# Placing the operands of the large matrix products at a fixed address distance in a two-layer decoder trunk

## The chip, the cores and the metric

The kernel runs on one core of one Trainium2 chip. The metric is the device time of one execution in microseconds. Three timed runs of the kernel before gave 616.25, 617.42 and 618.36 us; the median is 617.42 us.

## The reference, cut to what matters

One sequence of 256 tokens by 1024 features passes two layers. Layer 0 mixes tokens with causal attention (16 heads of 64), layer 1 with an mLSTM (8 heads); each is followed by a SwiGLU feed-forward part of width 2816. All of it is float32.

```python
def swiglu(xn, w_gate_up, w_down):
    gu = jnp.einsum('bsd,df->bsf', xn, w_gate_up)
    g, u = gu[..., :D_FF], gu[..., D_FF:]
    return jnp.einsum('bsf,fd->bsd', jax.nn.silu(g) * u, w_down)
...
    for i in range(DEPTH):
        j = i // N_MIXERS
        if i % N_MIXERS == 0:
            h = h + moba_mixer(rmsnorm(h, attn_norm[j]), attn_w_qkv[j], attn_w_o[j], cos, sin)
        else:
            h = h + mlstm_mixer(rmsnorm(h, mlstm_norm[j]), mlstm_w_in[j], mlstm_b_gates[j],
                                mlstm_head_norm[j], mlstm_w_out[j])
        h = h + swiglu(rmsnorm(h, ffn_norm[i]), ffn_w_gate_up[i], ffn_w_down[i])
    return rmsnorm(h, final_norm)
```

## The kernel before

Every float32 factor a is split exactly into a high part and a low part of the type float32r, and a product is made of three matmuls, high by high, high by low and low by high (`mm3`, line 176, through `mm`, line 173, so that nearly all matmuls have line 174). The weights come as 196 units of [128, 1024] in the order of use: the DMA queue of SP fills one of four buffers `raw`, ScalarE (ACT) casts it to `wh`, VectorE (DVE) subtracts to get `wl` (`prefetch`, line 139; `low`, line 135). There are eight buffers each of `wh` and `wl`. A unit feeds 24 matmuls of 256 columns or 12 of 512.

A matmul has a stationary operand (128 columns, brought in by a weight load, the engine PEld in the profile) and a moving operand (256 or 512 columns here). Which side the weights are on differs by phase:

- `first_block` (line 246) and `pair_block` (line 235): the weights are stationary and the normalised input `xh`, `xl` moves, 256 columns. This is the query/key part of both mixers (units `aqk`, `mqk`) and all gate and up products (`gu0`, `gu1`). In each feed-forward part `first_block` makes 192 matmuls and 18 chunks of `pair_block` make 48 each, 1056 together; they write tiles `ps`, one chunk per layer a tile `acc`.
- `out_tiles` (line 330): weights stationary, 256 columns move: `oh`, `ol` after attention (`ao`), `yh`, `yl` after the mLSTM (`mout`), `hh`, `hl` in the down product of layer 0 (`d0`), 24 matmuls a K tile. They write tiles `acc`.
- `tok_block` (line 267, the value and gate inputs `av`, `mv`, `mo`) and `tok_tiles` (line 393, the down product `d1` of layer 1): the input or `hh`, `hl` is stationary and the weights move, 512 columns, 12 matmuls a unit or K tile.

In the two mixer phases the work of the heads (small matmuls, softmax, gates) is put between steps of the large products at places written down by hand (`Stream`, line 279). In the feed-forward phases the chunks and the down products follow each other: a chunk of 48 matmuls, then a K tile of the down product. The order on TensorE is the order of the code; that on the other engines is written out in the attention phase and made by the scheduler elsewhere.

Where tiles lie in the on-chip memory SBUF follows from the sizes of the pools and tiles, one behind the other. Of interest is the start of an operand within 256 bytes; all offsets inside these tiles that the large products use are multiples of 512 bytes. In the built program before:

| operand | start, bytes modulo 256 |
|---|---|
| `xh`, `xl` | 0 |
| `wh`, `wl` | 32 |
| `hh`, `hl`; `oh`, `ol` | 224 |
| `yh`, `yl` | 32 |

So the distance D, start of the stationary operand less start of the moving one, modulo 256, is 32 in `first_block` and `pair_block`, 64 in `d0` and `ao`, 0 in `mout`, 224 in `tok_block` and 192 in `d1`.

Of the kernel before, what the change touches and what calls it, by code (L numbers as in the profile page):

```python
# [9 lines left out]
F32 = mybir.dt.float32  # L10
F32R = mybir.dt.float32r
# [5 lines left out]
P = 128  # L17
S = 256
NF = 8
NJ = 22  # L20
EPS = 1e-6
# weights: units prepared ahead, buffers, K tiles between a hidden tile and its use
LOOK = 4
# [6 lines left out]
WARM = 16  # L30
# where the pieces of the heads come, in steps of the large products
A_D1, A_X, A_D2, A_N, A_D3, A_L, A_D4, A_O1, A_O2 = 0.5, 1, 3, 1, 1, 1.5, 0.5, 1, 1
# [3 lines left out]

# columns of the constant tables
C_COS, C_SIN, C_AMASK, C_ID = 0, 256, 512, 768
C_EMASK, C_TRIU, C_TRIS, C_ID2, C_END = 896, 1152, 1280, 1408, 1416
# columns of the small vectors  # L40
V_ATTN, V_FFN0, V_MLSTM, V_FFN1, V_HEAD, V_BIAS, V_END = 0, 8, 16, 24, 32, 40, 56


def unit_names():
    """The order in which the units of weights (name, index, half) are used."""
    def each(name, ids):
        return [(name, i, h) for i in ids for h in range(2)]

    def outer(name):
        return [(name + "*", k, 0) for k in range(NF)]  # L50

    def a_units():
        n, v = [], each("av", range(4))
        parts = {0: [v[0:4]], 1: [v[4:4 + V1 // 4], v[4 + V1 // 4:]]}
        for i in ORDER:
            n += parts[i].pop(0) if i < 4 else each("aqk", [i])
        return n

    def ffn(l):
        n = outer(f"gu{l}")  # L60
        nd = 0
        for j in range(4, NJ):
            while nd <= j - LAG and j >= 6:
                n.append((f"d{l}", nd // 2, nd % 2))
                nd += 1
            n += each(f"gu{l}", [j])
        return n + [(f"d{l}", i // 2, i % 2) for i in range(nd, NJ)]

    n = outer("aqk") + a_units() + each("ao", range(4)) + ffn(0)
    n += outer("mqk") + each("mv", (0, 1)) + each("mo", (0, 1)) + each("mv", (2, 3)) + each("mo", (2, 3))  # L70
    n += each("mout", range(4)) + ffn(1)
    return n
# [3 lines left out]
def trunk_kernel(ctx: ExitStack, tc: tile.TileContext, x, w, wg, fw, tab, out):  # L76
    nc = tc.nc
    names = unit_names()
    index = {n: i for i, n in enumerate(names)}

    const = ctx.enter_context(tc.tile_pool(name="const", bufs=1))
    raw_pool = ctx.enter_context(tc.tile_pool(name="raw", bufs=RAW))
    w_pool = ctx.enter_context(tc.tile_pool(name="wsplit", bufs=WBUFS))
# [21 lines left out]
    nc.scalar.activation(dummy, warm[:, 0:1], AF.Exp)  # L105

    XV = xp.tile([P, V_END + NF * S], F32, name="XV")
    vt = XV[:, 0:V_END]
    X = XV[:, V_END:].rearrange("p (f t) -> p f t", f=NF)
    tab_t = const.tile([P, C_END], F32, name="tab_t")  # L110

    # weights: a stream of units [128, 1024], split exactly into two float32r parts
    raws = []
    split = {}
# [24 lines left out]
    def prefetch(upto, lag=0):  # L139
        for c in range(len(split), min(upto, len(names))):  # L140
            load(c + RAW - 1)
            wh = w_pool.tile([P, 1024], F32R, name="wh", tag="wh")
            wl = w_pool.tile([P, 1024], F32R, name="wl", tag="wl")
            split[c] = (wh, wl)
# [31 lines left out]
    def mm3(o, a, b, start, stop):  # L176
        """o += a^T b for exactly split a = (ah, al), b = (bh, bl)."""
        mm(o, a[0], b[0], start, False)
        mm(o, a[0], b[1], False, False)
        mm(o, a[1], b[0], False, stop)  # L180

    class Norm:
        """The split x * w, and the row scale 1/rms that is applied to what the products give."""

# [13 lines left out]
        def square(self, f):  # L198
            """Squares of the tiles f and f + 1."""
            xs = X[:, f:f + 2].rearrange("p f t -> p (f t)")  # L200
# [18 lines left out]
        def rows(self):  # L219
            pb = acc_tile()  # L220
            for t in range(2):
                nc.tensor.transpose(pb[:, t * P:(t + 1) * P], self.r[:, t:t + 1].to_broadcast([P, P]), ident)
            self.R = sm.tile([P, S], F32, name="R", tag="R")
            nc.scalar.copy(self.R, pb[:, 0:S])
# [10 lines left out]
    def pair_block(name, i, n, bank):  # L235
        """Products of one [8K, 2 x 128] chunk, 128 features by 256 tokens each."""
        for k in range(NF):
# [8 lines left out]
    def first_block(name, n):  # L246
        """The first four chunks of a phase with the K tiles outermost: the products start as soon as the
        first K tile of x is there."""
        banks = [ps_tile() for _ in range(4)]
# [17 lines left out]
    def tok_block(name, i0, n, evict, later):  # L267
        """x-stationary product [tokens, 512 columns] over two chunks."""
        banks = [acc_tile() for _ in range(2)]
# [9 lines left out]
    class Stream:  # L279
        """The large products of a phase in small steps, between which the work of the heads is put: each  # L280
        piece at the number of steps that it comes after."""

# [13 lines left out]
        def when(self, pos, ready, f, *args):  # L296
            """f at pos, or after it as soon as ready() holds."""
            def attempt():
# [31 lines left out]
    def out_tiles(acc, u, rhs, first, last, fs=range(NF)):  # L330
        """acc[f] += W[f]^T rhs for one K tile."""
        for f in fs:
# [4 lines left out]
    def out_steps(acc, name, i, src):  # L337
        """The output products of K tile i in four steps."""
        u, rhs = unit(name, i // 2, i % 2), src.pop(i)
# [4 lines left out]
    def out_start(acc, name, src):  # L344
        """The output products of the first two K tiles, by two banks at a time."""
        steps = []
# [14 lines left out]
    def finish(acc, steps, col):  # L361
        """The last output products, by bank, and the next norm's operands as the banks end."""
        n = Norm(col)
# [12 lines left out]
    def tok_tiles(acc, u, h, t, c, last):  # L376
        """acc[t, c] += h^T W for one K tile, tokens by features."""
        sl, cs = slice(t * P, (t + 1) * P), slice(c * 512, (c + 1) * 512)
        mm3(acc[2 * t + c], (h[0][:, sl], h[1][:, sl]), (u[0][:, cs], u[1][:, cs]), False, last)

    def finish_last(acc, steps, fwb, fp):
        """The last output products and the final norm, tokens by features."""
        for t in range(2):
# [21 lines left out]

# [1 line left out]
    n = n0 = Norm(V_ATTN)  # L407
# [19 lines left out]
    def stacks(pool, mv, bufs, ubufs=2, later=None):  # L427
        """mv: [m | a] of two heads. Per head [[mh, ah, ml], [ml, al, mh]], so that two products over the
        128 rows give all of a^T m."""
        u = pool.tile([P, 1024], F32R, name="u", tag="u", bufs=ubufs)  # L430
# [22 lines left out]
    with ExitStack() as actx:  # L453
# [5 lines left out]
        nc.gpsimd.tensor_mul(Cr, tcos, n.R)  # L459
        nc.gpsimd.tensor_mul(Sr, tsin, n.R)  # L460
        VT = ap1.tile([P, 2, 16, P], F32R, name="VT")
        swap = [8 + i if i < 8 else i - 8 if i < 16 else i for i in range(32)]
# [19 lines left out]
        def v_evict(n0, banks, part=0):  # L482
            # per head pair [vh0, vl0, vl1, vh1]
            for t in range(2):
# [50 lines left out]
        def transposes(h):  # L535
            pt = pr.pop(h)
            tp = ps_tile()
            # (k0, q0), (k0, q1), (k1, q1)
            for i in range(3):
# [78 lines left out]

# [1 line left out]
    def ffn(l, n, fp, col):  # L620
# [25 lines left out]
        def down(j):  # L646
            u = unit(f"d{l}", j // 2, j % 2)
            if not acc:
                acc.extend(acc_tile() for _ in range(4))
                if last_phase:  # L650
                    # the residual seeds the sums
                    for b in range(4):
# [32 lines left out]

# [1 line left out]
    with ExitStack() as mctx:  # L687
        mp = mctx.enter_context(tc.tile_pool(name="ml", bufs=2))
        m1 = mctx.enter_context(tc.tile_pool(name="ml1", bufs=1))
        VV = m1.tile([P, 2, 8, 258], F32R, name="VV")  # L690
        nc.gpsimd.memset(VV[:, :, :, 128:129].bitcast(F32), 1.0)
# [11 lines left out]

        # gates
        gp = acc_tile()
# [20 lines left out]
        def gates_1():  # L726
# [16 lines left out]
            z = m1.tile([P, 2, 8], F32, name="gz")  # L743
            # log1p(e) = 2 atanh(e / (2 + e)), |e / (2 + e)| <= 1/3
            nc.vector.tensor_scalar(d, e, 2.0, None, op0=ALU.add)
# [47 lines left out]
        def heads_e(h):  # L793
# [3 lines left out]
            E = mp.tile([P, 384], F32, name="E", tag="E", bufs=2)  # L797
            # (s1, t1), (s0, t0), (s0, t1)
            for i, b in enumerate((1, 0, 2)):
# [21 lines left out]
        def heads_b(h, t):  # L821
            # h / sqrt(mean(h^2) + eps) with h = num / den is num / sqrt(mean(num^2) + eps den^2)
            if t == 0:
                hpre[h] = (mp.tile([P, 2, 129], F32, name="hpre", tag="hpre", bufs=2),
                           sm.tile([P, 8], F32, name="hsc", tag="hsc", bufs=3))
# [39 lines left out]
        def o_evict(i, banks):  # L865
            # sigmoid(v) = (1 + tanh(v / 2)) / 2
            rh = sm.tile([P, 2], F32, name="rh", tag="rh")
# [135 lines left out]
```

## Time and profile before

| | |
|---|---|
| median of three timed runs | 617.42 us |
| span of the profiled execution, first to last instruction | 614.8 us |
| TensorE busy with matmuls (PE) / weight loads (PEld) | 601.1 us (98%) / 571.5 us (93%) |
| VectorE / ScalarE / GpSimd busy | 417.1 us / 340.7 us / 76.9 us |
| matmuls in the trace | 4524 |
| share of the span on PE, chain that ended last | 80% |

The 2.6 us between span and median lie around the span, in the launch and its end. Matmuls are pipelined: the trace gives each a duration of some 0.28 us (256 columns), but they start closer together than that. What a product costs is the distance from one start to the next, and the chain that ended last, which counts a matmul from the start of one to the start of the next, shows it: its pieces give a start, a length and the number of instructions.

### The profile page before, as it was taken

How to read it: one execution, taken by the hardware profiler on the slowest of the kernel's cores; microseconds unless marked ns; L12 is line 12 of the kernel's file. 1: busy time of each engine (PE TensorE's matmuls, PEld its weight loads, DVE VectorE, ACT ScalarE, POOL GpSimd, SP SyncE). 2: the span in 40 equal slices, each digit the busy share in tenths (PEclk: the TensorE clock that was granted, in tenths of full speed). 3: DMA queues.
4: the chain of work that ended last, by engine and by line, in shares of the span. 5: the costliest groups of instructions: out<-in, count | busy, mean ns of one | idle time of the engine just before them, and what ended most of it. 6: DMA issues, size and time to landing. Idle time of an engine off the chain costs nothing.

```text
span 614.8 us, 11568 instructions
## 1 busy us (share of the span) xinstructions
PE 601.1 (98%) x4524; PEld 571.5 (93%) x4524; DVE 417.1 (68%) x663; ACT 340.7 (55%) x611; POOL 76.9 (13%) x76
## 2 busy tenths in 40 slices
PE   8997999999999999999999999999999999999995
PEld 7987999999999999999999778899999999999984
DVE  5899898788765656566477677867676565656532
ACT  7645999677544444444275368856564444444422
POOL 2573320051000000000032300112200000000000
PEclk9999999999999999999999999999999999999999
DMA  8878965558555556555528758442865565655401
GB/s 312 281 216 266 248 191 156 168 187 285 184 199 177 200 174 200 177 198 179 172 69 298 225 198 224 154 138 73 298 212 172 176 200 176 199 177 201 142 0 68
DMA packets 36342, 116.39 MB, mean 189 GB/s; under 512 B 4544, under 2 KB 7360, under 8 KB 36288
## 3 DMA queue, kind: packets, MB, share of 16 engines
q1 hardware_dynamic: 36288, 115.66, 58.2%
q8 instruction: 35, 0.57, 0.4%
q14 instruction: 19, 0.16, 0.1%
HBM read 105.15 MB, written 1.05 MB: 173 GB/s over the span
## 4 chain that ended last, share of the span: by engine, by line
PE 80%; DMA 5%; DVE 5%; issue 3%; ACT 3%; POOL 2%; SPq 2%; POOLq 0%; ACTq 0%; DVEq 0%
PE ps L174 44%; PE acc L174 34%; DMA raw<-w 4%; DVE wl L137 2%; DMA stk<-u 1%; PE ps L540 1%; DVE u L435 1%; ACT wh L147 1%; DVE xl L195 1%; ACT xh L194 1%; DVE mqk L700 0%; POOL gpoly L753 0%; POOL sh L472 0%; POOL qk L473 0%; SPq L439 0%
## 5 line engine op out<-in xcount | busy, mean ns | idle before, releaser
L137 DVE TENSOR_TENSOR wl<-raw,wh 128x1024 fp32r<-128x1024 f32 (+2 forms) x199 | 244.8, 1236 | 114.8 <-ACT wh L147 111.9
L147 ACT CAST wh<-raw 128x1024 fp32r<-128x1024 f32 (+2 forms) x199 | 205.4, 1038 | 195.1 <-PE ps L174 108.2
L174 PE MATMUL ps<-xh,wh 128*128 128x256 f32 x864 | 245.1, 284 | 0.6 <-ACT wh L147 0.6
L174 PE MATMUL ps<-xh,wl 128*128 128x256 f32 x864 | 243.9, 282 | 0.5 <-DVE wl L137 0.5
L174 PE MATMUL ps<-xl,wh 128*128 128x256 f32 x864 | 243.4, 282 | 0.0
L174 PEld LDWEIGHTS ps<-xh,wh 128*128 128x128 f32 x864 | 163.6, 189 | 1.6 <-ACT wh L147 0.8
L174 PEld LDWEIGHTS ps<-xl,wh 128*128 128x128 f32 x864 | 163.8, 190 | 0.7
L174 PEld LDWEIGHTS ps<-xh,wl 128*128 128x128 f32 x864 | 163.6, 189 | 0.9 <-DVE wl L137 0.9
L174 PE MATMUL acc<-hh,wh 128*128 128x256 f32 x176 | 48.9, 278 | 0.0
L174 PE MATMUL acc<-hl,wh 128*128 128x256 f32 x176 | 48.8, 277 | 0.0
L174 PE MATMUL acc<-hh,wl 128*128 128x256 f32 x176 | 48.7, 277 | 0.0
L207 POOL TENSOR_TENSOR ssum<-ssum,sq 128x512 f32<-128x512 f32 x12 | 20.8, 1735 | 204.2 <-issue 169.4
L629 DVE TENSOR_TENSOR tgu<-ps,R 128x512 f32<-128x512 f32 x42 | 28.6, 690 | 23.8 <-PE ps L174 23.8
L174 PE MATMUL acc<-wh,xh 128*128 128x512 f32 x96 | 39.4, 411 | 0.0
L174 PE MATMUL acc<-wl,xh 128*128 128x512 f32 x96 | 38.0, 395 | 0.0
L174 PE MATMUL acc<-wh,xl 128*128 128x512 f32 x96 | 37.9, 395 | 0.0
L174 PE MATMUL acc<-wh,hl 128*128 128x512 f32 x88 | 34.7, 394 | 0.0
L174 PE MATMUL acc<-wl,hh 128*128 128x512 f32 x88 | 34.5, 392 | 0.0
L174 PE MATMUL acc<-wh,hh 128*128 128x512 f32 x88 | 34.2, 389 | 0.0
L174 PEld LDWEIGHTS acc<-hh,wh 128*128 128x128 f32 x176 | 33.2, 188 | 0.0
L174 PEld LDWEIGHTS acc<-hh,wl 128*128 128x128 f32 x176 | 33.1, 188 | 0.0
L174 PEld LDWEIGHTS acc<-hl,wh 128*128 128x128 f32 x176 | 33.0, 188 | 0.0
(179 smaller groups left out, 853.4 us busy)
## 6 DMA issues: line engine op xcount, KB each, us to landing
raw<-w SPq DMA_DIRECT2D x195, 512.0 KB, 3.4
stk<-u SPq DMA_DIRECT2D x24, 192.0 KB, 4.4
stk<-u SPq DMA_DIRECT2D x24, 128.0 KB, 4.3
stk<-u SPq DMA_DIRECT2D x24, 64.0 KB, 3.7
out<-yout SPq DMA_DIRECT2D x4, 256.0 KB, 2.2
XV<-x SPq DMA_DIRECT2D x7, 128.0 KB, 6.2
tab_t<-tab SPq DMA_DIRECT2D x1, 708.0 KB, 6.9
fwb<-fw SPq DMA_DIRECT2D x1, 512.0 KB, 3.4
```

The costliest lines, as they stand in the source:

```text
L137: nc.vector.tensor_sub(wl[:, sl], raws[c][:, sl], wh[:, sl].bitcast(F32))
L147: nc.scalar.copy(wh[:, sl], raws[c][:, sl])
L174: nc.tensor.matmul(o, lhsT=lhsT, rhs=rhs, start=start, stop=stop, skip_group_check=True)
L194: nc.scalar.activation(self.h[:, f], X[:, f], AF.Copy, scale=wc)
L195: nc.vector.scalar_tensor_tensor(out=self.l[:, f], in0=X[:, f], scalar=wc, in1=self.h[:, f].bitcast(F32), op0=ALU.mult, op1=ALU.subtract)
L207: nc.gpsimd.tensor_add(self.ssum, self.ssum, sq)
L435: nc.vector.tensor_sub(u[:, 512:1024], mv, u[:, 0:512].bitcast(F32))
L540: nc.tensor.transpose(tp[:, i * P:(i + 1) * P], pt[:, i * P:(i + 1) * P], ident)
L629: nc.vector.tensor_mul(t.rearrange("p (g t) -> p g t", g=2), bank.rearrange("p (g t) -> p g t", g=2), n.R2())
```

## The change

The tiles are moved so that D is 64 in all of the large products. Four things do this: unused pad tiles of 56, 56, 8, 16 and 48 float32 per partition push later tiles on, each with a memset of one column on GpSimd; the buffers of `wh` and `wl` have 1088 columns instead of 1024, of which the units whose weights move (`av`, `mv`, `mo`, `d1`) use 1024 from column 32 on and the others from column 0; the tile `R` has one buffer instead of two; the rows of `hpre` are 144 long instead of 129. Comments are removed, which shifts the line numbers.

```diff
+MOVING = ("av", "mv", "mo", "d1")
...
     const = ctx.enter_context(tc.tile_pool(name="const", bufs=1))
+    pad_pool = ctx.enter_context(tc.tile_pool(name="pad", bufs=1))
+
+    def pad(pool, n):
+
+        t = pool.tile([P, n], F32, name=f"pad{len(pads)}", bufs=1)
+        nc.gpsimd.memset(t[:, 0:1], 0.0)
+        pads.append(t)
+
+    pads = []
+    pad(pad_pool, 56)
...
+    pad(xp, 56)
+    pad(sm, 8)
     XV = xp.tile([P, V_END + NF * S], F32, name="XV")
...
-            wh = w_pool.tile([P, 1024], F32R, name="wh", tag="wh")
-            wl = w_pool.tile([P, 1024], F32R, name="wl", tag="wl")
+            o = 32 if names[c][0] in MOVING else 0
+            wh, wl = (w_pool.tile([P, 1088], F32R, name=a, tag=a)[:, o:o + 1024] for a in ("wh", "wl"))
...
-            self.R = sm.tile([P, S], F32, name="R", tag="R")
+            self.R = sm.tile([P, S], F32, name="R", tag="R", bufs=1)
...
+        pad(ap1, 16)
         VT = ap1.tile([P, 2, 16, P], F32R, name="VT")
...
+        pad(m1, 48)
         VV = m1.tile([P, 2, 8, 258], F32R, name="VV")
...
-                hpre[h] = (mp.tile([P, 2, 129], F32, name="hpre", tag="hpre", bufs=2),
+                hpre[h] = (mp.tile([P, 2, 144], F32, name="hpre", tag="hpre", bufs=2)[:, :, 0:129],
```

In the built program after, `xh`, `xl`, `hh`, `hl`, `oh`, `ol`, `yh` and `yl` start at 192 modulo 256, and the weights at 0 where they are stationary and at 128 where they move. D is 64 in every product of `first_block`, `pair_block`, `out_tiles`, `tok_block` and `tok_tiles`. The products of the heads with the tile `stk` on both sides keep D = 0. Instructions and their order are the same on every engine but GpSimd. There the five memsets are added; the first rows of its order before are these (`warm` is the operand of the warm-up matmuls, the rest are constants):

```order
L995 MEMSET const-uint8-127 128x1
L999 UNCONDITIONAL_BRANCH
L100 MEMSET warm 128x256
L169 MEMSET meancol 128x1
L171 MEMSET mhalf 128x2
L425 MEMSET AR 128x384
```

After the change three of the pads stand around `warm` and a fourth behind `AR`:

```order
L1014 MEMSET const-uint8-127 128x1
L1018 UNCONDITIONAL_BRANCH
L92 MEMSET pad_61 128x1
L115 MEMSET warm 128x256
L92 MEMSET pad_104 128x1
L92 MEMSET pad_106 128x1
L186 MEMSET meancol 128x1
L188 MEMSET mhalf 128x2
L442 MEMSET AR 128x384
L92 MEMSET pad_466 128x1
```

One memset now stands ahead of the one that the warm-up waits for; the fifth, not shown, stands ahead of the memsets of `VV` in the mLSTM phase.

## Rows read from the trace of the kernel before

**Rows 1.** The page's busy times: engine, us, share, instructions.
```profile
PE 601.1 (98%) x4524; PEld 571.5 (93%) x4524; DVE 417.1 (68%) x663; ACT 340.7 (55%) x611; POOL 76.9 (13%) x76
```
**Rows 2.** Busy time by stretch: PE, PEld, DVE, ACT, POOL, granted clock, DMA share, GB/s.
```profile
117.00:318.00 201.00, 201.00 (x1719) 201.00 (x1719) 130.35 (x164) 101.09 (x145) 12.17 (x10) 1.00 0.55 184
...
416.00:608.00 192.00, 192.00 (x1381) 181.28 (x1380) 114.54 (x145) 88.14 (x128) 8.63 (x6) 1.00 0.48 162
```
**Rows 3.** Chain that ended last: start us, length us, instruction and count.
```profile
221.50 5.67 PE ps L174 x48
227.17 2.75 PE acc L174 x24
...
294.59 14.33 PE acc L174 x126
...
415.81 5.04 PE acc L174 x42
420.84 14.20 PE ps L174 x120
...
465.77 2.75 PE acc L174 x12
...
592.17 13.75 PE acc L174 x60
```
**Rows 4.** Timeline of PE, down product of layer 0: start us, duration us.
```profile
299.90 0.28 PE L174 MATMUL acc<-hh,wh 128*128 128x256 f32 x1
...
303.98 0.28 PE L174 MATMUL acc<-hh,wh 128*128 128x256 f32 x1
```
**Rows 5.** Timeline of all engines in the same stretch.
```profile
299.98 1.05 ACT L147 CAST wh<-raw 128x1024 fp32r<-128x1024 f32 x1 [1.37 <-PE acc L174]
...
300.01 0.19 PEld L174 LDWEIGHTS acc<-hh,wl 128*128 128x128 f32 x1
```
**Rows 6.** Timeline of PE, `tok_block` of the mLSTM.
```profile
338.06 0.39 PE L174 MATMUL acc<-wl,xh 128*128 128x512 f32 x1
...
340.62 0.39 PE L174 MATMUL acc<-wh,xh 128*128 128x512 f32 x1
```
**Rows 7.** Timeline of PE, attention phase.
```profile
62.08 0.41 PE L174 MATMUL ps<-xh,wh 128*128 128x256 f32 x1
...
63.36 0.41 PE L174 MATMUL ps<-xh,wh 128*128 128x256 f32 x1
```
**Rows 8.** Busy time by stretch there (columns as in rows 2).
```profile
62.00:63.00 1.00, 1.00 (x7) 1.00 (x6) 0.68 (x5) 1.00 (x4) 0.92 (x2) 0.50 1.07 196
```
**Rows 9.** Groups of PE: names, shapes, count, busy us, mean ns, idle us.
```profile
L174 PE MATMUL ps<-xh,wh 128*128 128x256 f32 x864 | 245.1, 284 | 0.6 <-ACT wh L147 0.6
...
L174 PE MATMUL acc<-hh,wh 128*128 128x256 f32 x176 | 48.9, 278 | 0.0
...
L174 PE MATMUL acc<-wh,xh 128*128 128x512 f32 x96 | 39.4, 411 | 0.0
...
L174 PE MATMUL acc<-wh,hh 128*128 128x512 f32 x88 | 34.2, 389 | 0.0
```
**Rows 10.** Waits of PE: total us, times, longest us.
```profile
PE ps L540 <- ACT p L530: 2.5, 1, 2.5
PE ps L174 <- DVE logf L756: 1.6, 1, 1.6
```
**Rows 11.** Chain that ended last, attention phase from 24 us.
```profile
40.97 3.78 DMA stk<-u
...
59.24 0.71 ACT p L530 x2
```
**Rows 12.** Chain that ended last, mLSTM phase from 335 us.
```profile
341.53 4.14 DMA stk<-u
...
353.99 0.19 DVE logf L756
```
**Rows 13.** Timeline of GpSimd at the start.
```profile
1.00 0.10 POOL L171 MEMSET mhalf<- 128x2 f32 x1
```

## The prediction

> **What bounds the kernel now.** I read the busy times first: PE is busy for 98% of the span, weight loads for 93%, no other engine for more than 68% [rows 1]. Matmuls overlap in the trace, so that alone would not show a bound. The chain that ended last does: from 117 to 308 us and from 413 to 606 us it is PE piece after PE piece (nearly all of it L174; the rest is a few transposes of the norm and the residual), and in these two stretches PE has no gap, VectorE is busy for 60 to 65% of the time and the DMA engines for about half [rows 2, 3]. There the time is the number of products times the distance between their starts. Waits of PE are few: one of 2.5 us in the attention phase and one of 1.6 us in the mLSTM phase are the only large ones [rows 10].
>
> Next I divided pieces of the chain by their counts, because they show the distance for three values of D at the same shape, 128 by 128 times 256 columns:
>
> - D = 64, down product of layer 0: 14.33 us for 126, 113.7 ns each [rows 3]. In the clean part of it, 36 starts lie between 299.90 and 303.98 us: 113.3 ns [rows 4].
> - D = 32, chunks of gate and up: 5.67 us for 48, 118.1 ns, and 14.20 us for 120 in `first_block`, 118.3 ns [rows 3].
> - D = 0, the output product of the mLSTM: 5.04 us for 42, 120.0 ns [rows 3].
>
> With 512 columns: D = 192 gives 2.75 us for 12 and 13.75 for 60, 229.2 ns [rows 3]; D = 224 gives 11 starts in 2.56 us, 232.7 ns [rows 6].
>
> What could the distance be at best? At 62 us the granted clock is 0.50, the 1.2 GHz level [rows 8], and six starts of 256 columns then take 1.28 us, 213.3 ns [rows 7]. Half of it, 106.7 ns, is what the columns alone take at 2.4 GHz, and 213.3 ns for 512. So a product costs more than its columns by 6.6 ns at D = 64, 11.6 at 32, 13.3 at 0, and of 512 columns by 15.9 at 192 and 19.4 at 224. At the low clock there is no such surcharge, and it is about the same whatever else runs: a cast by ScalarE starts at 299.98 us, inside the 113.3 ns stretch [rows 4, 5]. The load of the next stationary operand starts with the current matmul (a load at 300.01 us [rows 5], the start 113 ns after 299.90 [rows 4]), so the two reads run side by side, and where their addresses stand to each other is a plausible cause.
>
> The best check on that is `out_tiles`: the down product of layer 0 (113.3 ns) and the output product of the mLSTM (120.0 ns) are the same code with the same shapes and the same use of the accumulators, and differ in D alone. `first_block` changes bank as often as `out_tiles` and has the 118.3 ns of `pair_block`, so the accumulation pattern doesn't explain it either.
>
> **The change part by part.** The order of instructions is unchanged, so only durations and distances can move.
>
> *Chunks and first blocks, D from 32 to 64.* I take the 113.3 ns of the same shape [rows 4]: 118.3 - 113.3 = 5.0 ns each. The two feed-forward parts have 2 x 1056 = 2112: 10.6 us. The mLSTM's `first_block`, 192: 1.0 us. Of the attention phase I count only the 84 after 60 us: 0.4 us. The groups of `xh` and `xl` with 864 each [rows 9], and 96 more into `acc`, are these 2688. Ends: no gain if D is not the cause, and 11.6 ns if all surcharge goes.
>
> *mLSTM output, D from 0 to 64.* 8 K tiles x 24 = 192, by 120.0 - 113.3 = 6.7 ns: 1.3 us.
>
> *Down product of layer 1, D from 192 to 64.* 22 K tiles x 12 = 264 (three groups of 88 [rows 9]). No row shows 512 columns at 64. The nearest rows are 229.2 ns at 192 (no gain) and the 6.6 ns surcharge of 256 columns, which gives 213.3 + 6.6 = 220 ns. I take 220: there is one weight load to a product in both, of the same 128 columns, and the surcharge of 512 columns is of the size of that of 256. 9.2 ns x 264 = 2.4 us; ends 0 and, with no surcharge, 4.2 us.
>
> *Value and gate inputs, D from 224 to 64.* Three groups of 96 [rows 9]. Of these 288, 48 in attention and 123 in the mLSTM come behind the two waits below: 171 x (232.7 - 220) = 2.2 us; ends 0 and 3.3 us.
>
> *Down product of layer 0.* D stays 64, but between two chunks a K tile takes 2.75 us for 24, 114.6 ns [rows 3]: its first products still start at distances of the chunk before. With one D throughout, 16 such pieces x 24 x 1.3 ns: 0.5 us.
>
> *What is swallowed.* Until 60 us the chain does not run through PE: rotary, stacks, the DMA to `stk`, and the softmax end with a normalisation at 59.24 us [rows 11], and PE waits 2.5 us for it [rows 10]. The 300 chunk products and 48 value products before that would save 300 x 5.0 + 48 x 12.7 = 2.1 us; PE then waits longer, and I count nothing. The gates of the mLSTM likewise: DMA to `stk` at 341.53, a polynomial on GpSimd, `logf` at 353.99 [rows 12], for which PE waits 1.6 us [rows 10]. 69 value and gate products ahead of it, 0.9 us, are not counted. If neither wait grows, 3.0 us come on top.
>
> *Pads, `R`, `hpre`.* A one-column memset takes 0.10 us on GpSimd [rows 13]; five make 0.5 us, of which only the first stands ahead of something that waits (the warm-up, which ends before the first weights are split). `R` with one buffer makes the next layer's copy wait for the last reader of the old one, and that is the last chunk's post-processing, a whole residual and norm earlier. Both cost 0; without that cover 0.1 us. The reader of `hpre` has the same number of elements.
>
> Sum: 10.6 + 1.0 + 0.4 + 1.3 + 2.4 + 2.2 + 0.5 = 18.4 us. The profiled span becomes 614.8 - 18.4 = 596.4 us; with the 2.6 us between span and median, 617.4 - 18.4 = 599.0 us.
>
> **The rivals.**
>
> *Address is not the cause: no change.* The three distances at 256 columns could come from what reads the results or from the phase. For it: the three values of D also sit in three phases. Against it: `out_tiles` at two distances, above. The time would be 617. The Trainium skill states a rule that speaks for this rival: "TensorE: Matmul & The Clock Gate", under "Step-by-step: what each phase is for", has the streaming operand and the weight load on two independent read ports, so that loading the next weights takes nothing from the running matmul. By that rule the time stays at 617; the rows at 113.3 and 120.0 ns do not agree with it. The same page, under "Wait — 56ns, not 53.3ns?", gives a floor of 2.5 ns a matmul at the full clock; the rows show 6.6 at best, at D = 64.
>
> *PE is faster and others take it back.* With 512 columns gaining nothing, and both mixer phases held by their head work, what is left is 10.6 + 1.0 + 0.5 = 12.1 us: 605.3 us. For it: in the mixer phases ScalarE and VectorE feed PE through long chains [rows 11, 12], and longer waits can bring the half clock, as after the wait before 60 us. A second such dip is priced by rows 7 and 8: some 20 products at 213 instead of 118 ns, 1.9 us. Against it: both feed-forward parts have gapless PE and idle feeders [rows 2]. The weights stay fed: a unit now lasts 24 x 113.3 = 2.72 us instead of 2.84, a rate up by 4% with the DMA engines half idle.
>
> *Slower.* Not D but where the moving operand lies sets the surcharge. `xh` and `xl` move from 0 to 192, away from both the 224 of the fast products and the 0 of the middling ones. If this place costs what the slowest product of this shape does (120.0 ns), the 2688 chunk products gain 1.7 ns each, 4.6 us, `hh` and `oh` rise too, 720 x 6.7 = 4.8 us: 627 us. It decides once chunk products take over 118.3 ns. Against it: `xh` at 0 and `yh` at 32 give 118.3 and 120.0, hardly apart.
>
> *Everything gains.* Waits don't grow, the dip at 60 us does not come, 512 columns lose their surcharge: 18.4 + 3.0 + 1.9 + about 1 us, 593 us.
>
> **How the numbers follow.** The forecast, 595 to 604, has 0.73; taken back, 604 to 610, 0.13; everything gains, 0.06; no change 0.05; slower 0.03. The predicted time is 599. The range 593.5 to 607 leaves out about 0.2. Three runs differ by 0.3%, about what a measurement can tell. Faster by more than that 0.92, within it 0.05, slower 0.03.
>
> **What would show it.** Chain pieces: 48 chunk products in 5.44 us instead of 5.67; 120 of `first_block` in 13.6 instead of 14.20; 42 of the mLSTM output in 4.76 instead of 5.04; 12 of the layer 1 down product in 2.64 instead of 2.75; layer 0's down pieces 2.72. The waits for ACT p L530 and DVE logf should grow by up to 2.1 and 0.9 us. I am wrong on the main step if the 48 stay above 5.6 us, and on 512 columns if the 12 stay at 2.75; if the mixer phases from 60 to 117 and from 354 to 416 us are no shorter, the head work bounds them.

## The result and the profile after

The changed kernel takes 607.71 us (median of four runs, 606.29 to 609.44), the kernel before 617.89 us beside it (616.25 to 618.95). The ratio is 0.9835, with a 95% interval of 0.9809 to 0.9860: faster by 1.65%, 10.2 us. The forecast was 599.0 us, with 593.5 to 607.0 as its range: a gain right in sign and too large by 8 us; the measured time lies outside the range. The span of the profiled execution went from 614.8 to 604.5 us.

The busy times of after, to set beside [rows 1]:

```profile
PE 588.8 (97%) x4524; PEld 556.7 (92%) x4524; DVE 415.9 (69%) x663; ACT 340.2 (56%) x611; POOL 77.2 (13%) x81
```

The chain of after that ended last (start us, length us, instruction and count), the pieces that answer to [rows 3]:

```profile
124.49 13.66 PE ps L191 x120
...
217.74 5.44 PE ps L191 x48
223.18 2.72 PE acc L191 x24
...
288.46 14.29 PE acc L191 x126
...
409.10 4.95 PE acc L191 x42
414.05 14.13 PE ps L191 x120
...
460.73 5.45 PE ps L191 x48
466.18 2.79 PE acc L191 x12
...
581.54 14.00 PE acc L191 x60
```

The main step came as forecast: 48 chunk products take 5.44 us in layer 0 and 5.45 in layer 1, where they took 5.67; layer 0's down pieces take 2.72. Three things did not. Layer 1's `first_block` (the 14.13) takes 117.8 ns a product, while the same code in layer 0 (the 13.66) takes 113.8. The output product of the mLSTM stands at 4.95, not 4.76. And layer 1's down product, with 512 columns, became slower: 2.79 for 12 against 2.75, 14.00 for 60 against 13.75.

The value and gate inputs gained nothing either. In the timeline of PE of after (start us, duration us) the first and the last of 19 starts stand 4.19 us apart, 232.8 ns each, against the 232.7 of [rows 6]:

```profile
331.61 0.39 PE L191 MATMUL acc<-wl,xh 128*128 128x512 f32 x1
...
335.80 0.40 PE L191 MATMUL acc<-wl,xh 128*128 128x512 f32 x1
```

The waits of PE in after (total us, times, longest us), to set beside [rows 10]:

```profile
PE ps L558 <- ACT p L548: 2.8, 3, 2.4
PE ps L191 <- issue: 1.7, 1, 1.7
PE ps L191 <- DVE logf L775: 1.3, 1, 1.3
```

The two known waits are about what they were. The third, 1.7 us, stands ahead of score products of the attention heads, and it has grown. In the timeline of PE it is the idle time in brackets, first after, then before:

```profile
55.24 0.69 PE L191 MATMUL ps<-stk 128*128 128x128 f32 x4 [1.65 <-issue]
```

```profile
54.80 0.70 PE L174 MATMUL ps<-stk 128*128 128x128 f32 x4 [0.52 <-PE ps L174]
```

Cutting both traces at the starts of the first matmuls of each part gives this, in us; the forecast is the sum of the prediction's terms for that part:

| part | before | after | shorter | forecast |
|---|---|---|---|---|
| attention phase | 124.8 | 124.3 | 0.5 | 1.0 |
| feed-forward part, layer 0 | 186.0 | 180.3 | 5.7 | 5.8 |
| mLSTM, `first_block` and gates | 25.2 | 24.9 | 0.3 | 1.0 |
| mLSTM, the rest | 84.7 | 84.4 | 0.3 | 2.9 |
| feed-forward part, layer 1 | 187.6 | 184.0 | 3.6 | 7.7 |
| final norm and store | 6.6 | 6.6 | 0 | 0 |

So 8 us of the 18.4 are missing, and they are missing in layer 1's feed-forward part (4.1) and in the mixer phases (3.8).

### The profile page after: what moved, and what is told of

Its sections match the earlier page's. It is cut to its first block, busy times and chain, and to the rows that moved or that the text cites. A ratio compares the mean times of both kernels' runs of the same rounds, so it can differ in the third digit from the quotient of the medians.

```text
span 604.5 us, 11573 instructions
## 1 busy us (share of the span) xinstructions
PE 588.8 (97%) x4524; PEld 556.7 (92%) x4524; DVE 415.9 (69%) x663; ACT 340.2 (56%) x611; POOL 77.2 (13%) x81
## 4 chain that ended last, share of the span: by engine, by line
PE 76%; DVE 6%; DMA 6%; issue 3%; ACT 3%; SPq 2%; POOL 2%; POOLq 0%; ACTq 0%; DVEq 0%
PE ps L191 42%; PE acc L191 33%; DMA raw<-w 4%; DMA stk<-u 3%; DVE wl L154 3%; DVE u L452 1%; PE ps L558 1%; ACT wh L164 1%; SPq L455 1%; SPq L456 1%; DVE xl L212 1%; ACT xh L211 1%; DVE VT L510 0%; DVE mqk L719 0%; POOL gpoly L772 0%
## 5 line engine op out<-in xcount | busy, mean ns | idle before, releaser
L191 PE MATMUL ps<-xh,wh 128*128 128x256 f32 x864 | 240.6, 278 | 0.9 <-ACT wh L164 0.9
L191 PE MATMUL ps<-xh,wl 128*128 128x256 f32 x864 | 239.7, 277 | 0.7 <-DVE wl L154 0.7
L191 PE MATMUL ps<-xl,wh 128*128 128x256 f32 x864 | 239.1, 277 | 0.0
L191 PEld LDWEIGHTS ps<-xh,wh 128*128 128x128 f32 x864 | 162.5, 188 | 2.1 <-ACT wh L164 1.1
L191 PEld LDWEIGHTS ps<-xh,wl 128*128 128x128 f32 x864 | 162.2, 188 | 1.5 <-DVE wl L154 1.5
L191 PEld LDWEIGHTS ps<-xl,wh 128*128 128x128 f32 x864 | 162.5, 188 | 0.7
L191 PE MATMUL acc<-hh,wh 128*128 128x256 f32 x176 | 48.6, 276 | 0.0
L191 PE MATMUL acc<-hl,wh 128*128 128x256 f32 x176 | 48.6, 276 | 0.0
L191 PE MATMUL acc<-hh,wl 128*128 128x256 f32 x176 | 48.6, 276 | 0.0
L191 PE MATMUL acc<-wh,xh 128*128 128x512 f32 x96 | 39.4, 411 | 0.0
L191 PE MATMUL acc<-wl,xh 128*128 128x512 f32 x96 | 37.9, 395 | 0.0
L191 PE MATMUL acc<-wh,xl 128*128 128x512 f32 x96 | 37.9, 395 | 0.0
L191 PE MATMUL acc<-wh,hh 128*128 128x512 f32 x88 | 34.8, 396 | 0.0
L191 PE MATMUL acc<-wh,hl 128*128 128x512 f32 x88 | 34.7, 395 | 0.0
L191 PE MATMUL acc<-wl,hh 128*128 128x512 f32 x88 | 34.7, 395 | 0.0
L191 PEld LDWEIGHTS acc<-hh,wl 128*128 128x128 f32 x176 | 33.0, 188 | 0.0
L191 PEld LDWEIGHTS acc<-hh,wh 128*128 128x128 f32 x176 | 33.0, 188 | 0.0
L191 PEld LDWEIGHTS acc<-hl,wh 128*128 128x128 f32 x176 | 33.0, 188 | 0.0
```

The costliest lines, as they stand in the source:

```text
L191: nc.tensor.matmul(o, lhsT=lhsT, rhs=rhs, start=start, stop=stop, skip_group_check=True)
```

## The experiments

Each ratio is to the kernel before, run on the same chip. In the pieces shown, L191 is the line of `mm` (L192 or L200 where a kernel has more lines above it).

### Is it the distance?

**A sweep in layer 1.** Each chunk gets its own distance, the moving operand staying at 192; the down products go through the same eight values.

```diff
+STEPS = (0, 96, 32, 192, 128, 224, 160, 64)
...
-            o = 32 if names[c][0] in MOVING else 0
+            o = offset(*names[c])
```

(For `gu1`, `offset` gives (STEPS[i % 8] - 64) % 256 // 4, for `d1` (192 - STEPS[(2 * i + h) % 8]) % 256 // 4.)

> The kernel after, with D running through eight values (0, 96, 32, 192, 128, 224, 160, 64) from chunk to chunk of the second feed-forward part (256 columns move) and from K tile to K tile of its down product (512 columns move); nothing else changes. Theory A (the surcharge is a matter of D, and the best D differs by the number of columns): 48 chunk products take 5.44 us at 64, 5.67 at 32 and 5.76 at 0; of 512 columns, 12 take about 2.79 us at 64 and 224, 2.75 at 192, and some other distance may be lower. Theory B (512 columns pay about the same wherever they lie): the 12 lie between 2.74 and 2.80 us at all eight distances. Theory C (the place of the moving operand decides, not D; it stays at 192 in the chunks here): 48 chunk products take 5.44 us at every D.

One run took 610.91 us, before 617.69. The chain, chunks 6 to 13, at D = 160, 64, 0, 96, 32, 192, 128 and 224 in this order:

```profile
453.45 5.75 PE ps L200 x48
...
462.01 5.66 PE ps L200 x48
...
470.47 5.75 PE ps L200 x48
...
479.01 5.63 PE ps L200 x48
...
487.44 5.67 PE ps L200 x48
...
495.91 5.66 PE ps L200 x48
...
504.37 5.69 PE ps L200 x48
...
512.86 5.60 PE ps L200 x48
```

The second round of eight gave the same lengths within 0.01 us. The distance matters, 119.8 ns at D = 0 and 160 against 116.7 at 224, at one phase, one code and one place of the moving operand. But D = 64 is not the 5.44 of the changed kernel here: 5.66, 117.9 ns. The same distance, and another time; and at 5.66 against the 5.67 of D = 32 there is nothing to gain. At 512 columns the K tiles of 12 took 2.76 to 2.81 us over all eight distances: nearly flat, with no good place at 64, and 2.80 at D = 192, where the kernel before had 2.75.

**The 512 columns back at D = 192.** `MOVING` is empty, so that weights that move start at 0.

```diff
-MOVING = ("av", "mv", "mo", "d1")
+MOVING = ()
```

> The kernel after, with no unit of weights moved by 32 columns, so that all 512-column products have D = 192 and the 256-column ones keep 64. Theory A: the down product of layer 1 goes back to 2.75 us for 12 (from 2.79), 22 x 0.04 = 0.9 us; the value and gate inputs go from 232.7 to about 229 ns, up to 0.6 us behind the waits: some 606.5 us, a span of 603. If the mixer phases are held by their head work, only the 0.9 us appear. Rival (what changed in the down product of layer 1 is not D): 2.79 us for 12 stay, 607.7 us.

610.89 us (608.72 to 612.97), ratio 0.9882 (0.9831 to 0.9933). The chain:

```profile
463.80 5.66 PE ps L191 x48
469.45 2.77 PE acc L191 x12
```

The down product got back half of what it had lost, 2.77, and the chunks, which nobody had touched, went from 5.45 to 5.66. So what stands ahead of a chunk changes its time. The value inputs at the start of attention did go to about 229 ns, as the theory had it (228.9 ns for 47 distances between starts, 233.2 in the changed kernel), but the attention phase took 124.6 us, no less than the 124.3 of after.

**All tiles 32 bytes further on,** all distances as in the changed kernel.

```diff
-    pad(pad_pool, 56)
+    pad(pad_pool, 64)
```

> The first pad is 64 instead of 56 columns, so that every later tile starts 32 bytes further on and all distances stay as in the changed kernel; the moving operand of the chunks is at 224 instead of 192. Theory (only the distance counts): 48 chunk products 5.44 to 5.46 us, 12 of the last down product 2.77 to 2.80 us, time within 2 us of the changed kernel. Rival (the place of the moving operand counts by itself): the 48 take 5.55 us or more.

One run took 608.49 us. The chain:

```profile
411.96 4.78 PE acc L191 x42
416.75 13.60 PE ps L191 x120
...
462.90 5.45 PE ps L191 x48
```

The place of the moving operand (224 instead of 192) doesn't count for the chunks, which the theory said. What it had not said: the mLSTM's output product and `first_block` now take the 4.78 and 13.60 that the forecast had for them. At D = 64 both can run at 113.3 or at 117.8 ns.

### Do the mixer phases take part?

**Mixers at the distances of before.** The units of both mixers go back to their old distances; the feed-forward parts stay.

```diff
-MOVING = ("av", "mv", "mo", "d1")
+OFFSET = {"aqk*": 56, "aqk": 56, "av": 56, "mqk*": 56, "mqk": 56, "mv": 56, "mo": 56, "mout": 48, "d1": 32}
...
-            o = 32 if names[c][0] in MOVING else 0
+            o = OFFSET.get(names[c][0], 0)
```

> The kernel after, with the weights of both mixer phases put back to the distances of before (32 in query and key, 224 in value and gate inputs, 0 in the mLSTM output); the feed-forward parts keep 64. Theory A (the head work holds the mixer phases): the time stays within 1 us of the kernel after, 607 to 608.7 us, and the waits on PE shrink by what its products lose. Rival (PE bounds them, and the gain there is real but was offset by something else): about 3 us slower, 610 to 611 us.

608.42 us (608.08 to 611.28), ratio 0.9858 (0.9819 to 0.9896): no difference from the changed kernel that could be measured. Nearly all of the gain is that of the feed-forward parts. The wait ahead of the score products is 0.9 us here, between the 0.5 of before and the 1.7 of after. That head work holds both phases is not shown by this run alone: the section on the prediction counts how little the products of these phases had gained, and so could lose.

**Later places for the head work.** Two runs move pieces of the head work in the order that is written by hand, so that they no longer wait: the gates of the mLSTM, and the start of the heads in attention.

```diff
-M_START, M_STEP, M_A, M_B, M_C, M_G2, M_G3 = 32, 5, 1.5, 12, 22, 23, 28
+M_START, M_STEP, M_A, M_B, M_C, M_G2, M_G3 = 32, 5, 1.5, 12, 22, 27, 30
```

> The kernel after, with the second and third piece of the mLSTM's gates put 4 and 2 steps later in the stream of large products (27 and 30 instead of 23 and 28), about 2.8 us of products. Theory A (the mixer phase swallows the gain because PE waits for logf, 1.3 to 3.5 us in the runs so far, and a long wait brings the half clock behind it): the wait for logf goes below 1 us, no half clock near 350 us, 1 to 3 us faster than the kernel after on its median, 605 to 607 us. Rival (the head work behind the gates sets the end of the phase, and the wait only moves to the first heads): no change, 607 to 609 us, with a new wait of PE between 355 and 365 us.

607.52 us (606.73 to 608.31), ratio 0.9826 (0.9798 to 0.9854). The waits of PE:

```profile
PE ps L807 <- DVE mrow L794: 1.9, 1, 1.9
...
PE ps L191 <- DVE AR L802: 1.0, 1, 1.0
```

The wait for `logf` is gone, two others of 2.9 us together stand in its place. The mLSTM phase took 110.2 us in this profile, 108.8 to 110.2 in three of the changed kernel: no shorter. That fits a stretch set by the chain of the gates and not by the products.

```diff
-A_START, A_STEP, A_T, A_V = 26, 3.0, 8, 14
+A_START, A_STEP, A_T, A_V = 29, 3.0, 8, 14
```

> The kernel after, with the attention heads started 3 steps later (29 instead of 26), about 2.1 us of large products more in front of the first scores. Theory A (PE waits for the first softmax because the heads start too early for the faster PE): the wait for ACT p falls from 2.4 or more to about 1 us, the half clock near 60 us goes away, 1 to 3 us faster, 605 to 607 us. Rival (the chain of head work ends the phase, and starting it later ends it later): 0 to 2 us slower, 608 to 610 us.

615.05 us (613.16 to 616.2), ratio 0.9945 (0.9923 to 0.9967). The attention phase grew by 4.6 us to 128.9; PE still waited 3.9 us in all for `p`. Here the heads bound the phase too: starting them later makes it longer.

### What sets one of the two times?

**Halves.** Layer 1's 512-column products are made as two of 256 columns.

```diff
-        sl, cs = slice(t * P, (t + 1) * P), slice(c * 512, (c + 1) * 512)
-        mm3(acc[2 * t + c], (h[0][:, sl], h[1][:, sl]), (u[0][:, cs], u[1][:, cs]), False, last)
+        sl = slice(t * P, (t + 1) * P)
+        for g in range(2):
+            cs = slice(c * 512 + g * S, c * 512 + (g + 1) * S)
+            mm3(acc[2 * t + c][:, g * S:(g + 1) * S], (h[0][:, sl], h[1][:, sl]), (u[0][:, cs], u[1][:, cs]),
+                False, last)
```

> The kernel after, with each 512-column product of the layer 1 down product made as two of 256 columns, with D = 64 and a weight load each. Theory A (256 columns at 64 cost 113.3 ns; 512 at 64 cost 232.6): 24 of them take 2.72 us instead of 2.79 for 12, 22 x 0.07 = 1.5 us, about 606.2 us. Rival (a weight load more per product costs its 6.6 ns and more, or the pattern falls into the 117.7 ns that D = 64 also shows in places): 2.82 us for 24, 608.5 us.

610.4 us (608.33 to 613.99), ratio 0.9885 (0.9835 to 0.9936). The chain:

```profile
465.86 5.65 PE ps L191 x48
471.51 2.74 PE acc L191 x24
```

The halves are quick, 114.3 ns (228.5 for 512 columns), and the chunks between them slow. **With the last product of a K tile left whole** (`w = 512 if t == c == 1 else S`), it is the other way round:

> The kernel with 512-column products of the layer 1 down product made in halves, but with the last three products of each K tile left at 512 columns, as in the kernel after. Theory R (at D = 64 there are two rhythms, 113.3 and 117.8 ns, and what stands just ahead of a stretch decides which one it falls into; three 512-column products at 64 lead to the fast one): 48 chunk products take 5.45 us again, the K tile about 2.74 us, and the second feed-forward part is 1 us shorter than in the kernel after. Rival (any halves in the K tile spoil the chunk behind them): 5.65 us for 48, and the part is 2 to 3 us longer than in the kernel after.

609.16 us (608.7 to 612.15), ratio 0.9863 (0.9829 to 0.9897). The chain, 18 halves and 3 whole products in the 21:

```profile
462.75 5.45 PE ps L191 x48
468.21 2.82 PE acc L191 x21
```

The chunks are quick again, the 18 halves now take 117.9 ns. At a switch between chunk and down product the next weight load stands at another distance from the operand that moves (0 one way, 128 the other), so the next theory was that this sets the rhythm.

**One distance throughout.** `hh` and `hl` of layer 1 start at 0 and the weights of `d1` at 192, so that D is 64 within and across the switches; with halves, and with whole products.

```diff
-            o = 32 if names[c][0] in MOVING else 0
+            o = 48 if names[c][0] == "d1" else 32 if names[c][0] in MOVING else 0
...
         if last_phase:
+            pad(fp, 16)
```

> Layer 1's down products are two of 256 columns each, and the tiles of that phase are placed so that hh and hl start at 0 and the moving weights at 192 modulo 256; the distance is 64 inside the chunks, inside the down products and also from each to the next at a switch. Theory (the rhythm is set at the switches, where the next weight load stood at another distance): chunks and down pieces both keep the quick rhythm, 48 in 5.44 to 5.46 us and 24 in 2.72 us, the part from the first chunk on some 1.7 us shorter than with 512 columns, median 605 to 607 us. Rival (the rhythm is set by the change of tiles or accumulators itself, not by the distance at the switch): the chunks take 5.65 us again as with halves before, median 609 to 611 us.

612.62 us (611.45 to 613.45), ratio 0.9900 (0.9862 to 0.9939). The chain:

```profile
445.72 5.45 PE ps L191 x48
...
452.91 2.83 PE acc L191 x24
455.74 5.65 PE ps L191 x48
...
588.59 14.15 PE acc L191 x120
```

> The placement of the run with one distance throughout, but with the 512-column products left whole. Theory (512 columns cost about 231 to 233 ns wherever they stand, since eight distances were flat): 12 take 2.77 to 2.80 us, chunks 5.44 to 5.46 us, the time of the changed kernel, 607 to 609 us. Rival (the 512-column products were slow only because each switch broke the distance, or because of where the weights lay): 12 take 2.64 to 2.72 us, median 605 to 606.5 us.

611.14 us (608.91 to 614.72), ratio 0.9886 (0.9825 to 0.9948); chunks 5.66, K tiles 2.79. The theory fell. Between 445.72 and 452.91 stand 16 transposes of the residual; from them on every product down to the end is slow, through 16 chunks at one distance. Nothing disturbs the rhythm, so it stays, as it does in the quick form in layer 0, at the same distance, with the same starts modulo 256.

**Disturbed units.** If the time is a state that lasts, a short stretch at another distance should be able to change it. In layer 0, the second unit (24 products) of five chunks is placed otherwise.

```diff
+KICK = {("gu0", 8, 1): 32, ("gu0", 11, 1): 48, ("gu0", 14, 1): 16, ("gu0", 17, 1): 56, ("gu0", 20, 1): 32}
...
-            o = 32 if names[c][0] in MOVING else 0
+            o = KICK.get(names[c], 32 if names[c][0] in MOVING else 0)
```

> The changed kernel, but in layer 0's feed-forward part the second unit of the chunks 8, 11, 14, 17 and 20 is placed otherwise, so that 24 products have D = 192, 0, 128, 32 and 192 in place of 64; everything else stays at 64. Theory (a stretch at another distance flips the rhythm): after the first disturbance the chunks take 5.65 us instead of 5.44, after the second 5.44, after the third 5.65, and so on. Rival A (the disturbance costs only itself, 24 products at 118 to 120 ns, 0.1 us each): all undisturbed chunks stay at 5.44 us. Rival B (what stood last decides, not the rhythm before): the two disturbances by D = 192 lead to the same rhythm.

One run took 608.57 us. The chain, with chunk 8 (D = 192), chunks 11 and 12 (0 in chunk 11), 14 (128), 17 and 18 (32 in chunk 17) and 20 (192):

```profile
177.35 5.44 PE ps L192 x48
...
201.83 5.60 PE ps L192 x48
...
210.26 5.65 PE ps L192 x48
...
227.22 5.68 PE ps L192 x48
...
252.68 5.66 PE ps L192 x48
258.34 2.74 PE acc L192 x24
261.08 5.44 PE ps L192 x48
...
277.40 5.44 PE ps L192 x48
```

This is the run that shows the state, in one execution. In the quick rhythm D = 192 can't be told from 64. Behind twenty-four products at D = 0 (119.9 ns) comes the slow rhythm, which stays for six chunks, also through 24 products at D = 128. Then 24 at D = 32 (118.2 ns) lead back, within four products, to 113.3 ns. Neither the flip at each disturbance nor rival A holds; the two at D = 192 agree with rival B, but both met the quick rhythm, so they don't prove it.

**The same in layer 1:** the run with one distance and halves, its first K tile at D = 128 or at D = 192.

```diff
-            o = 48 if names[c][0] == "d1" else 32 if names[c][0] in MOVING else 0
+            o = 32 if names[c] == ("d1", 0, 0) else 48 if names[c][0] == "d1" else 32 if names[c][0] in MOVING else 0
```

(16 instead of the first 32 for D = 192.)

> The run with one distance throughout and halves, but the first K tile of layer 1's down product (24 products) at D = 128. Theory (such a stretch flips the rhythm): the slow rhythm that came with the residual's transposes is left, the chunks behind it take 5.44 to 5.46 us and the down pieces 2.72, median 605 to 607.5 us. Rival (the rhythm of this part is set by something else): chunks 5.65 us, 611 to 614 us as without it.

607.44 us (606.31 to 609.44), ratio 0.9816 (0.9762 to 0.9869). The chain:

```profile
452.21 2.88 PE acc L191 x24
455.10 5.45 PE ps L191 x48
460.55 2.72 PE acc L191 x24
```

> As the run with the first K tile at D = 128, but D = 192. Theory (any other distance flips it): chunks behind it 5.44 to 5.46 us, down pieces 2.72, median 605 to 607.5 us. Rival (the distance of the disturbance decides): the two runs differ, one in the slow rhythm at 611 to 614 us, the other in the quick one.

612.48 us (610.27 to 615.34), ratio 0.9899 (0.9862 to 0.9935). The chain:

```profile
452.57 5.65 PE ps L191 x48
```

The rival of the second run held. These two kernels differ in where one unit lies, 24 of 4788 matmuls, and by 5.6 us in layer 1's feed-forward part (182.6 and 188.2 us); their medians, over four and eight runs, stand 5.0 us apart. Rival B of the disturbed units falls here too: D = 192 stood last in both runs, and each time the rhythm is the one that it met.

**The last two questions:** does a stretch at D = 32 also help behind the mLSTM, and are 512 columns quicker in the quick rhythm? To the kernel with D = 128 in its first K tile a disturbed last unit of `mout` is added (`("mout", 3, 1): 56`); the kernel with one distance and whole products gets one disturbed unit (`("gu1", 6, 1)` from column 56 on). The changed kernel ran along.

> The run with halves, one distance throughout and a first K tile at D = 128, and now also the last unit of the mLSTM's output product at D = 32 (24 products). Theory (a stretch at D = 32 leads from the slow rhythm into the quick one, as in layer 0): first_block of layer 1 takes 13.60 to 13.65 us for 120 instead of 14.13, the part behind it stays quick (48 in 5.44, 24 in 2.72), median 605.5 to 607.5 us, 0.5 us under the run without it. Rival (it only did so by chance): first_block stays at 14.13 us.

607.3 us (606.1 to 608.76), ratio 0.9825 (0.9789 to 0.9862). `first_block` stayed slow:

```profile
416.55 14.14 PE ps L192 x120
```

> The run with one distance throughout and whole 512-column products, which went through the last part in the slow rhythm, and now the second unit of chunk 6 at D = 32 (24 products). Theory (512 columns have the two rhythms too, and the changed kernel ran them in the slow one): behind the disturbance the chunks take 5.44 to 5.46 us and 12 of the down product 2.72 to 2.75 us (229 ns or less) instead of 2.79. Rival (512 columns cost 232 to 233 ns at this distance in either rhythm): chunks 5.44 to 5.46, the 12 stay at 2.79 us.

One run took 610.04 us. The chain around chunk 6, which starts at 456.06:

```profile
456.06 5.67 PE ps L191 x48
...
464.53 5.45 PE ps L191 x48
469.98 2.79 PE acc L191 x12
```

The disturbance led the chunks into the quick rhythm, and the 12 stay at 2.79: no quick form of 512 columns shows at this distance (rival). And D = 32 is no rule: it led out of the slow rhythm twice and once not.

The changed kernel ran twice more, in two sets.

> The kernel after once more, on the same chip as the other three of this set. If the length of the mixer phases varies from execution to execution with the half clock, the span lies between 604 and 609 us, and the lengths of the two feed-forward parts are the same as in the first profile to 0.2 us.

> The changed kernel again, beside the fastest version: 607 to 608 us, chunks 5.45, 12 of the last down product 2.79, first_block of layer 1 14.13 us.

607.96 us (605.65 to 608.74), ratio 0.9838 (0.9807 to 0.9868), and 608.84 us (605.06 to 610.74), ratio 0.9845 (0.9806 to 0.9883). The two versions with halves and a disturbed K tile (607.44, 607.30) have the shortest layer 1, 182.6 us against 184.0. In the total that is not shown: beside the changed kernel on one chip 607.30 stands against 608.84, with ranges that overlap.

## Why the prediction was right in sign and wrong in size

**Chunks and first blocks: right.** 10.6 us were forecast for the 2112 products of the feed-forward parts. The chunks went to 113.3 to 113.8 ns (5.44 to 5.46 us for 48), and layer 0's part became 5.7 us shorter, of 5.8. Only layer 1's `first_block` missed its share, and with it layer 1's products of `xh` and `xl` gave 4.5 us instead of 5.3.

**The down product of layer 1: the step that failed most.** "I take 220" rested on the surcharge of 256 columns and on no row of 512. Measured are 232.5 ns, and eight distances are nearly flat. The term was +2.4 us and is -1.0: the 229.2 ns of the kernel before are the lowest that any run shows for this product, and the change left them, outside the two ends that the prediction gave. The error was in the bounds: 229.2 ns was one of only two distances seen, so a loss belonged in the range.

**Value and gate inputs: the same step.** 232.8 ns for 232.7; the 2.2 us are 0.

**The mLSTM's output product and layer 1's `first_block`: the mechanism was incomplete.** The working took 113.3 ns as what D = 64 costs. It is what D = 64 costs in one of two rhythms; the other is 117.8, and after the mLSTM the profiles of after have the slow one. 1.3 us became about 0.5 in starts, and `first_block` gave 0.07 us on its 120. The kernel before had a row that shows this, and the prediction has it nowhere: the attention output is `out_tiles` too, with D = 64 and the same starts modulo 256 as layer 0's down product, and the chain of before has it so:

```profile
117.11 7.83 PE acc L174 x66
```

The last 65 starts, 117.12 to 124.66 us, stand 117.8 ns apart, not 113.3. So `out_tiles` had two times at one distance, and the "best check", which compared only its two other uses, could not lay their difference to D alone. In after the distance of this product is the same, and it is quick:

```profile
116.94 7.55 PE acc L191 x66
```

**The mixer phases: mostly the same step, and less the rival's.** Forecast were 4.9 us in three rows of the table, measured 1.1. Most of these products did not get as cheap as the working had it. From start to start, with gaps and half clock left out, the mLSTM's query/key products went from 118.3 to 115.0 ns, its output product from 119.4 to 116.6, attention's chunks after 60 us from 118.0 to 116.7, and the value and gate inputs stayed at 233: 0.6, 0.5, 0.1 and 0 us, some 1.3 of the 4.9. The attention output gave 0.3 us that nobody had forecast. What is left for the head work to take back is about half a microsecond. So the undone mixers had little to lose. For attention the traces do show the head work: the products ahead of the score products became quicker, the wait there grew from 0.5 to 1.7 us, and PE went on behind the wait for `p` at 59.87 us, where it had been 59.60. That is the gain which the prediction had not counted; its signature was put at the wrong place, as the waits for `p` and `logf` (2.8 and 1.3 us, from 2.5 and 1.6) did not grow by the 2.1 and 0.9 us. For the mLSTM it is argued only, from the waits that came back elsewhere. The half clock of [rows 7, 8] is not in this profile of after; it is in its second one, whose attention phase is no longer (124.1 us), and in its third, where it lasts some 10 us and the phase takes 125.9 us.

**The accounting.** 18.4 - 10.3 = 8.1 us are missing: 3.4 in the down product of layer 1, 3.8 in the mixer phases, 0.7 to 0.8 in layer 1's products of `xh` and `xl`. Nearly all of it is one step, the cost of a product at D = 64. The rival "PE is faster and others take it back", 605.3 us within 604 to 610, has the time, with 512 columns a loss instead of nothing; of its two conditions the first came, and the second, head work, took little. That the time lies in its range is in part luck. It had 0.13 and deserved more, since its first condition could be read in the rows: none stood for 512 columns at 64. The rival "everything gains" was added up wrongly: 512 columns without surcharge are 2.9 us by the prediction's own ends, not about 1, and the time 591 us, not 593.

**No change, and slower.** If the address were not the cause, the time would have been 617 us. The disturbed units tell against that rival most plainly: in one phase and one code, a product took 113.3 ns at D = 64 and 119.9 at D = 0. The Trainium skill, "TensorE: Matmul & The Clock Gate", "Step-by-step: what each phase is for", has the two reads independent; the runs here don't agree with it. The rival "slower", by the place of the moving operand, fell with the shifted tiles: 5.45 us at 224 as at 192.

## What to carry to other kernels

Where PE is gapless, the distance between starts is the cost, and it can hang on where the operands lie: place them, and look at the chain's pieces, not at the busy time. A gain read at one shape should not be carried to another shape without a row; give the term a loss as its lower end. And before a duration is multiplied by a thousand products, look whether the same instruction at the same starts stands at a second duration somewhere (here the attention output, 117.8 ns beside the 113.3 that were taken), and count no gain in a phase that other engines' chains bound.

## What was not expected of the hardware

The two rhythms: 256 columns at D = 64 with a weight load each start every 113.3 or every 117.8 ns, for hundreds of products without change. Small matmuls between them (transposes, the mean of the norm) or a stretch at D = 0, 32 or 128 can lead from one to the other. D = 192 led nowhere in three cases: it kept the quick rhythm twice and the slow one once. Placement and order of the instructions do not settle the rhythm alone. Layer 0's `first_block` took 13.66 us for 120 in the profile of after; in four runs whose edits lie behind it (the gates later, the two with one distance, the disturbed units) it was slow. The run with disturbed units has the same instructions at the same starts up to there:

```profile
124.40 14.16 PE ps L192 x120
```

Which way a disturbance goes, and why, stays open; that it hangs on how the reads of the next weights and of the moving operand meet is only argued.

The half clock has a second place, early in the mLSTM phase, in some of the profiles. In the run with `MOVING` empty PE waits 3.5 us for `logf`, and then the busy times by stretch (columns as in [rows 2]) show the clock near its 1.2 GHz level for 3.6 us:

```profile
350.00:353.60 3.60, 3.60 (x14) 2.80 (x14) 2.93 (x7) 2.85 (x4) 0.00 (x0) 0.53 0.39 146
```

The mLSTM's rest took 87.1 us in that run and 84.4 in the profiled run of after, which has no such stretch. The length of this wait alone doesn't settle it: the run with the mixers as before waited 2.5 us for `logf` without one, and that with the last product left whole 1.5 us with one.
